# Average pooling 2x2: store packets grown from 16 KB to 63.5 KB per partition, and moved from a queue of their own into the loads' queue

## Chip, cores, metric

The kernel runs on one core of one Trainium2 chip; the other cores are idle. The metric is the device time of one execution in microseconds. All timed runs quoted here are in the fast state, and the core's clock is 1.0 in all of them, so no run had to be set aside; the four probes ran once each, so their state is unknown. The runs were spread over several chips; the kernel before, timed beside each batch, stayed at 3106.4 to 3106.5 us. Ratios are the mean time of one kernel's runs over the mean of the other's in the same rounds, with a 95% interval; they are not quite the ratio of the medians that are quoted. The span of a profile is about 1.7 us shorter than the time of the same execution.

## The reference

```python
x: float32 [32, 128, 256, 256]; kernel_size = 2; stride = 2
for i in range(128):
    for j in range(128):
        output[:, :, i, j] = mean(x[:, :, 2*i:2*i+2, 2*j:2*j+2], axis=(2, 3))
```

1,073.7 MB are read and 268.4 MB are written. Two input rows (2 KB) give one output row (512 bytes); I call this a unit. There are 4,096 units for each of the 128 partitions. A packet is what one DMA engine moves at a time: here one partition's share of a transfer, so a transfer has 128 packets, eight for each of the 16 engines (a load takes 19.3 us, one of its packets 2.42).

## The kernel before

The input is one list of units. A load takes 32 units for each partition: 64 KB per partition, 8 MB in all, one block in HBM. VectorE (DVE) adds the row pairs in place, then the column pairs; ScalarE (ACT) multiplies by 0.25; the result, 16 KB per partition, is stored. Loads are issued by SyncE (SP), stores by ACT: two hardware queues, which share the core's 16 DMA engines.

```python
sbuf = ctx.enter_context(tc.tile_pool(name="sbuf", bufs=2))
for parts in plan:                       # 126 whole loads, then a cut-up tail
    in_tile = sbuf.tile([P, G_MAIN, s * w], f32, name="in_tile")   # 64 KB
    for g in parts:
        xt = xv[r0 : r0 + rows].rearrange("(p g) f -> p g f", p=P)
        ot = ov[r0 : r0 + rows].rearrange("(p g) f -> p g f", p=P)
        ...                              # it = this part of in_tile
        nc.sync.dma_start(out=it, in_=xt)
        nc.vector.tensor_add(...)        # row pairs, in place   (L87)
        col_sum = sbuf.tile([P, G_MAIN, w_out], f32, name="col_sum", bufs=3)
        nc.vector.tensor_add(...)        # column pairs          (L96)
        nc.scalar.mul(out=col_sum[:, :g], in_=col_sum[:, :g], mul=inv)   # L108
        nc.scalar.dma_start(out=ot, in_=col_sum[:, :g])
```

## Time and profile before

| | before |
|---|---|
| time, median of 4 runs | 3106.39 us (3106.34 to 3106.69) |
| span of the profile | 3104.8 us |
| DMA over the span | 432 GB/s |
| one period (load, store, compute) | 24.2 us for 10.49 MB |
| DVE and ACT for one load | 8.69 + 4.43 us, and 3.62 us |

From the page of the kernel before: the engines' busy time, what DMA moved in each fortieth of the span, the two queues, and the three costliest groups (busy time and mean of one, then the idle time before them and what ended it).

```profile
span 3104.8 us, 1126 instructions
DVE 1681.4 (54%) x272; ACT 465.8 (15%) x137; POOL 0.2 (0%) x4
...
GB/s 418 436 439 425 436 439 425 436 438 429 433 439 430 431 439 434 427 439 435 426 438 436 427 437 436 428 436 437 427 436 437 428 436 437 429 435 437 432 431 396
...
q1 hardware_dynamic: 19584, 1073.75, 79.8%
q10 hardware_dynamic: 19584, 268.44, 20.2%
...
L87 DVE TENSOR_TENSOR in_tile<-in_tile 128x8192 f32<-128x8192 f32 (+4 forms) x136 | 1113.9, 8190 | 1406.7 <-DMA in_tile<-in_x_dram 1406.7
L108 ACT ACTIVATE col_sum<-col_sum 128x4096 f32<-128x4096 f32 (+4 forms) x136 | 464.5, 3415 | 2635.9 <-DVE col_sum L96 2635.9
L96 DVE TENSOR_TENSOR col_sum<-in_tile 128x4096 f32<-128x4096 f32 (+4 forms) x136 | 567.8, 4175 | 13.9 <-DMA out_dram<-col_sum 1.8
```

No slice of DMA is poor, and DVE waits 1,407 us in all for loads: the kernel is bound by DMA. The means of these groups mix shapes; the table has those of the full shape. One period in the timeline (start, duration, then the wait before):

```profile
1010.38 8.69 DVE L87 TENSOR_TENSOR in_tile<-in_tile 128x8192 f32<-128x8192 f32 x1 [10.97 <-DMA in_tile<-in_x_dram]
1019.17 4.43 DVE L96 TENSOR_TENSOR col_sum<-in_tile 128x4096 f32<-128x4096 f32 x1
...
1027.27 0.34 ACTq L110 DMA_DIRECT2D out_dram<-col_sum  x1
1034.57 8.69 DVE L87 TENSOR_TENSOR in_tile<-in_tile 128x8192 f32<-128x8192 f32 x1 [10.97 <-DMA in_tile<-in_x_dram]
```

The row adds start 24.19 us apart, so a load and a store of one period move at 10.49 MB / 24.19 us = 433.5 GB/s. The end of the kernel is poorer. Windows (stretch, length, busy times, clock, DMA share, GB/s):

```profile
3080.00:3090.00 10.00, 6.20 (x4) 1.87 (x2) 0.00 (x0) 1.00 0.99 419
3090.00:3100.00 10.00, 7.23 (x8) 2.33 (x4) 0.00 (x0) 1.00 0.82 332
3100.00:3104.80 4.80, 0.58 (x2) 0.63 (x3) 0.00 (x0) 1.00 0.33 111
```

In the last 24.8 us DMA moves (419 x 10 + 332 x 10 + 111 x 4.8) = 8.0 MB, worth 18.5 us at 435.2 GB/s (the most that the prediction below reckons with; it says where the figure comes from): 6.3 us are lost there. This view counts each packet whole in the window in which it starts, so short windows err at their edges.

### The profile page before, as it was taken

The page shows a single profiled execution, that of the slowest core. Times are in us where ns is not written, and L with a number is a line of the kernel's source. Part 1 is how long each engine was busy: PE and PEld are TensorE (multiplying, and loading weights), DVE is VectorE, ACT ScalarE, POOL GpSimd, SP SyncE. Part 2 cuts the span into 40 slices and gives each one's busy share as a digit, 9 for nine tenths or more (in the row PEclk, how much of TensorE's full clock was granted, in tenths as well). Part 3 has the DMA queues.
Part 4 walks back from the last instruction along what each step waited for, and adds up shares of the span by engine and source line. Part 5 has one row for each costly group of instructions (what it writes and reads, how often), then busy time and mean ns, then how long its engine had stood idle before and what let it go on. Part 6 is the DMA issues. An engine that isn't in the chain of part 4 may idle for free. (4 is left out here: it accounts for less than half of the span.)

```text
span 3104.8 us, 1126 instructions
## 1 busy us (share of the span) xinstructions
DVE 1681.4 (54%) x272; ACT 465.8 (15%) x137; POOL 0.2 (0%) x4
## 2 busy tenths in 40 slices
DVE  4555555555555555555555555555555555555556
ACT  1111111111111111111111111111111111111112
POOL 0000000000000000000000000000000000000000
DMA  9999999999999999999999999999999999999999
GB/s 418 436 439 425 436 439 425 436 438 429 433 439 430 431 439 434 427 439 435 426 438 436 427 437 436 428 436 437 427 436 437 428 436 437 429 435 437 432 431 396
DMA packets 39176, 1342.26 MB, mean 432 GB/s; under 512 B 4352, under 2 KB 4736, under 8 KB 5888
## 3 DMA queue, kind: packets, MB, share of 16 engines
q1 hardware_dynamic: 19584, 1073.75, 79.8%
q10 hardware_dynamic: 19584, 268.44, 20.2%
q14 instruction: 8, 0.07, 0.0%
HBM read 1073.74 MB, written 268.44 MB: 432 GB/s over the span
## 5 line engine op out<-in xcount | busy, mean ns | idle before, releaser
L87 DVE TENSOR_TENSOR in_tile<-in_tile 128x8192 f32<-128x8192 f32 (+4 forms) x136 | 1113.9, 8190 | 1406.7 <-DMA in_tile<-in_x_dram 1406.7
L108 ACT ACTIVATE col_sum<-col_sum 128x4096 f32<-128x4096 f32 (+4 forms) x136 | 464.5, 3415 | 2635.9 <-DVE col_sum L96 2635.9
L96 DVE TENSOR_TENSOR col_sum<-in_tile 128x4096 f32<-128x4096 f32 (+4 forms) x136 | 567.8, 4175 | 13.9 <-DMA out_dram<-col_sum 1.8
L108 ACT ACT_TABLE_LOAD x1 | 1.3, 1283 | 0.7 <-PEq L190 0.7
L190 POOL MEMSET const-bfloat16-1.0<- 128x1 bf16 x1 | 0.1, 102 | 0.0
L190 POOL MEMSET const-uint8-127<- 128x1 uint8 x1 | 0.1, 102 | 0.0
L190 POOL MEMSET const-float32-0.0<- 128x1 f32 x1 | 0.1, 99 | 0.2 <-issue 0.2
L190 POOL MEMSET const-float32-1.0<- 128x1 f32 x1 | 0.1, 99 | 0.0
## 6 DMA issues: line engine op xcount, KB each, us to landing
out_dram<-col_sum ACTq DMA_DIRECT2D x126, 2048.0 KB, 31.6
in_tile<-in_x_dram SPq DMA_DIRECT2D x5, 2048.0 KB, 27.5
in_tile<-in_x_dram SPq DMA_DIRECT2D x1, 4096.0 KB, 25.5
out_dram<-col_sum ACTq DMA_DIRECT2D x5, 512.0 KB, 12.0
in_tile<-in_x_dram SPq DMA_DIRECT2D x126, 35.1
out_dram<-col_sum ACTq DMA_DIRECT2D x1, 1024.0 KB, 12.7
in_tile<-in_x_dram SPq DMA_DIRECT2D x1, 1024.0 KB, 16.2
in_tile<-in_x_dram SPq DMA_DIRECT2D x1, 512.0 KB, 16.9
```

What stands on the lines that cost most here:

```text
L87: nc.vector.tensor_add(out=it[:, :, 0:w], in0=it[:, :, 0:w], in1=it[:, :, di * w : (di + 1) * w],)
L96: nc.vector.tensor_add(out=col_sum[:, :g], in0=it[:, :, 0:wu:s], in1=it[:, :, 1 : wu + 1 : s],)
L108: nc.scalar.mul(out=col_sum[:, :g], in_=col_sum[:, :g], mul=inv)
L190: nc = _bacc.Bacc("TRN2", target_bir_lowering=False, num_devices=1)
```

## The change

The intent: fewer and larger transfers, each in one direction for some 19 us, with no small stores mixed in packet by packet; and a tail whose compute hides beside the last big store. A group is now 127 units, loaded in four pieces of 31, 32, 32 and 32 units. All results of a group gather in one buffer and leave as one store of 63.5 KB per partition. To make that one run in HBM, a partition owns 127 units in a row, so the rows that one load reads lie 254 KB apart; before they lay 64 KB apart. The store goes into SP's queue behind the next group's first load, by when its data are ready. The diff, cut to its core:

```diff
-    for parts in plan:
-            nc.sync.dma_start(out=it, in_=xt)
-            ...
-            nc.scalar.dma_start(out=ot, in_=col_sum[:, :g])
+IN_UNITS = 32
+GROUP = 127
+FIRST = GROUP - 3 * IN_UNITS            # 31
+    res = out_pool.tile([P, GROUP + FIRST, w_out], f32, name="res")
+    for k in range(groups):              # 32 groups
+        xt = xv[r0 : r0 + GROUP * P].rearrange("(p g) f -> p g f", p=P)
+        ot = ov[r0 : r0 + GROUP * P].rearrange("(p g) f -> p g f", p=P)
+        base = 0 if k % 2 == 0 else FIRST
+        ...                              # pieces of the group, first the one of 31 units
+        for i, (a, g) in enumerate(pieces):
+            t = in_pool.tile([P, IN_UNITS, 2 * w], f32, name="in_tile")
+            nc.sync.dma_start(out=t[:, :g], in_=xt[:, a : a + g])
+            if i == 0 and last:
+                nc.sync.dma_start(out=last[0], in_=last[1])
+            pool(t[:, :g], res[:, base + a : base + a + g], [g] if i < 3 else [g - 8, 8])
+        last = (ot, res[:, base : base + GROUP])
+    ...   # tail, 32 units: three loads, then the last big store on SP, then
+          # compute and three small stores on ACT's queue beside it
```

More of the change, by code (lines that the diff above doesn't have):

```diff
@@ L27 @@
     R = n * c * h_out
-    if k == s and 2 <= k <= 4 and R > 0 and R % P == 0:
-        _nonoverlap_pool(ctx, tc, x, out, k, n, c, h, w, h_out, w_out)
+    units = R // P if R % P == 0 else 0
+    if k == 2 and s == 2 and h % 2 == 0 and w == 256 and units >= 1024:
+        _pool_2x2(ctx, tc, x, out, units)
     else:
         _generic_pool(ctx, tc, x, out, k, s, n, c, h, w, h_out, w_out)
-def _nonoverlap_pool(ctx, tc, x, out, k, n, c, h, w, h_out, w_out):
+IN_UNITS = 32
+GROUP = 127
+FIRST = GROUP - 3 * IN_UNITS
@@ L36, in _nonoverlap_pool, with _pool_2x2 @@
+def _pool_2x2(ctx, tc, x, out, units):
     nc = tc.nc
     P = nc.NUM_PARTITIONS
-    s = k
-    R = n * c * h_out
-    hv = h_out * s
-    xs = x if hv == h else x[:, :, 0:hv, :]
-    xv = xs.rearrange("n c (ho a) w -> (n c ho) (a w)", a=s)
-    ov = out.rearrange("n c ho wo -> (n c ho) wo")
-    assert xv.shape == (R, s * w) and ov.shape == (R, w_out)
-    wu = w_out * s
-    unit_bytes = s * w * 4
-    G_MAIN = max(1, min(R // P, (64 * 1024) // unit_bytes))
-    total_units = R // P
-    nmain, rem_units = divmod(total_units, G_MAIN)
@@ L54, in _nonoverlap_pool @@
-    plan: list[list[int]] = [[G_MAIN] for _ in range(nmain)]
-    if rem_units:
-        plan.append([rem_units])
-    if G_MAIN % 32 == 0 and nmain >= 4 and rem_units == 0:
-        u = G_MAIN // 32
-        tail = [
-            [16 * u, 8 * u, 8 * u],
-            [8 * u, 8 * u, 8 * u, 4 * u, 2 * u, u, u],
-        ]
-        assert all(sum(t) == G_MAIN for t in tail)
-        plan = plan[:-2] + tail
-    sbuf = ctx.enter_context(tc.tile_pool(name="sbuf", bufs=2))
-    inv = 1.0 / float(k * k)
@@ L71, in _nonoverlap_pool @@
-    r0 = 0
-    for parts in plan:
-        in_tile = sbuf.tile([P, G_MAIN, s * w], mybir.dt.float32, name="in_tile")
-        g0 = 0
-        for g in parts:
-            rows = P * g
-            xt = xv[r0 : r0 + rows].rearrange("(p g) f -> p g f", p=P)
-            ot = ov[r0 : r0 + rows].rearrange("(p g) f -> p g f", p=P)
-            r0 += rows
-            it = in_tile[:, g0 : g0 + g]
-            g0 += g
-            nc.sync.dma_start(out=it, in_=xt)
-            for di in range(1, k):
-                nc.vector.tensor_add(
-                    out=it[:, :, 0:w],
-                    in0=it[:, :, 0:w],
-                    in1=it[:, :, di * w : (di + 1) * w],
-                )
-            col_sum = sbuf.tile(
-                [P, G_MAIN, w_out], mybir.dt.float32, name="col_sum", bufs=3
-            )
-            nc.vector.tensor_add(
-                out=col_sum[:, :g],
-                in0=it[:, :, 0:wu:s],
-                in1=it[:, :, 1 : wu + 1 : s],
-            )
-            for dj in range(2, k):
-                nc.vector.tensor_add(
-                    out=col_sum[:, :g],
-                    in0=col_sum[:, :g],
-                    in1=it[:, :, dj : wu + dj : s],
-                )
-            nc.scalar.mul(out=col_sum[:, :g], in_=col_sum[:, :g], mul=inv)
-            nc.scalar.dma_start(out=ot, in_=col_sum[:, :g])
-        assert g0 <= G_MAIN
@@ L113, in _nonoverlap_pool, with pool @@
-    assert r0 == R, (r0, R)
+    f32 = mybir.dt.float32
+    w = x.shape[3]
+    w_out = w // 2
+    xv = x.rearrange("n c (ho a) w -> (n c ho) (a w)", a=2)
+    ov = out.rearrange("n c ho wo -> (n c ho) wo")
+    in_pool = ctx.enter_context(tc.tile_pool(name="inp", bufs=2))
+    out_pool = ctx.enter_context(tc.tile_pool(name="outp", bufs=1))
+    res = out_pool.tile([P, GROUP + FIRST, w_out], f32, name="res")
+    def pool(it, dst, cuts):
+        nc.vector.tensor_add(out=it[:, :, 0:w], in0=it[:, :, 0:w], in1=it[:, :, w:])
+        a = 0
+        for g in cuts:
+            d, v = dst[:, a : a + g], it[:, a : a + g]
+            nc.vector.tensor_add(out=d, in0=v[:, :, 0:w:2], in1=v[:, :, 1:w:2])
+            nc.scalar.mul(out=d, in_=d, mul=0.25)
+            a += g
@@ new lines, in _pool_2x2 @@
+    groups, rest = divmod(units, GROUP)
+    if rest == 0:
+        groups, rest = groups - 1, GROUP
+    last = None
+    for k in range(groups):
+        r0 = k * GROUP * P
+        xt = xv[r0 : r0 + GROUP * P].rearrange("(p g) f -> p g f", p=P)
+        ot = ov[r0 : r0 + GROUP * P].rearrange("(p g) f -> p g f", p=P)
+        base = 0 if k % 2 == 0 else FIRST
+        spans = [(FIRST + i * IN_UNITS, IN_UNITS) for i in range(3)]
+        if base == 0:
+            pieces = [(0, FIRST)] + spans
+        else:
+            pieces = [(3 * IN_UNITS, FIRST)] + [(a - FIRST, g) for a, g in spans]
+        for i, (a, g) in enumerate(pieces):
[5 more added lines that the diff above has]
+        last = (ot, res[:, base : base + GROUP])
@@ new lines, in _pool_2x2 @@
+    r0 = groups * GROUP * P
+    while rest:
+        n = min(rest, IN_UNITS)
+        t = in_pool.tile([P, IN_UNITS, 2 * w], f32, name="in_tile")
+        tout = in_pool.tile([P, IN_UNITS, 2 * w], f32, name="in_tile")
+        to = tout[:].rearrange("p g f -> p (g f)").rearrange("p (g f) -> p g f", f=w_out)
+        cuts = [n // 2, n // 4, n - n // 2 - n // 4] if n >= 8 else [n]
+        a, parts = 0, []
+        for g in cuts:
+            xt = xv[r0 : r0 + g * P].rearrange("(p g) f -> p g f", p=P)
+            ot = ov[r0 : r0 + g * P].rearrange("(p g) f -> p g f", p=P)
+            nc.sync.dma_start(out=t[:, a : a + g], in_=xt)
+            parts.append((ot, a, g))
+            a += g
+            r0 += g * P
+        rest -= n
+        if rest == 0:
+            nc.sync.dma_start(out=last[0], in_=last[1])
+        for ot, a, g in parts:
+            pool(t[:, a : a + g], to[:, a : a + g], [g])
+            nc.scalar.dma_start(out=ot, in_=to[:, a : a + g])
```

## The prediction

> **What bounds the kernel now.** The DMA engines, throughout. The page's 40 slices show DMA at 9 tenths everywhere, mean 432 GB/s; DVE is busy 54%, ACT 15%. By shape, an 8 MB load costs DVE 8.69 + 4.43 us and ACT 3.62 us; the timeline repeats every 24.20 us (row adds at 66.85 and 3043.27 us are 123 periods apart), of which DVE waits 11 us for a load. A period moves 8.389 + 2.097 MB: 433.3 GB/s. The Trainium skill, "DMA: Bandwidth & Descriptors", section "Where 436 GB/s comes from", puts the ceiling at 435.2. The trace agrees: the second load, no store beside it, lands 19.32 us after the first (42.02 - 22.70), 434.2 GB/s. In the packets, 64 KB take 2.418 us and 16 KB 0.611 us: 27.2 GB/s per engine plus about 9 ns a packet. All bytes at 435.2 GB/s need an estimated 3084 us, so no schedule wins more than some 20 us (0.7%).
>
> **Where those 20 us are.** 3.4 us before the first load flows and lands (22.70 - 19.32); about 13 us of packet cost (24.20 against 24.09 us a period; some 6 ns for each of 34,800 data packets); about 5 us at the end, where the windows 3090 to 3100 and 3100 to 3105 us show DMA shares of 0.82 and 0.31.
>
> **What the change does.** Loads stay 64 KB per partition (one in four 62 KB). Stores grow from 16 to 63.5 KB: store packets fall from 16,128 to 4,096, all data packets to about 21,200. At 6 to 9 ns over 16 engines that saves 5 to 7 us. Bytes and compute are unchanged; DVE and ACT have slack.
>
> *Does the one queue run dry?* Let a group's last load land at T. DVE needs 13.1 us, ACT's last call (8 units) 1.06: the store can be issued at T + 15. The next group's first load, issued at about T - 6, occupies the engines until T + 18.7, so the store is some 4 us early. The load behind it needs a buffer freed at T + 13.5, and the store runs until T + 38. I see no starved moment.
>
> *Tail.* The last big store needs about 19 us of DMA; the last compute (2.3 + 1.2 + 1.1 us) and the small stores (2 MB) hide beside it. Some 3.5 of the 5 us come back.
>
> **Sum, an estimate.** A group of 127 units: 41.6 MB / 435.2 GB/s = 95.64 us, + 40 packets x 6 ns = 95.9. Then 3.4 + 32 x 95.9 + 24.2 (rest) + 1.5 (last landing) + 1.6 (time over span before) = 3099.5 us. The saving is on the critical path, but only about 7 us, 0.2%.
>
> **Predicted: 3099 us, 3093 to 3106.** Faster by over 2%: 0.5%; within 2%: 98%; slower by over 2%: 1.5%.
>
> **What would show it.** Right: about 95.9 us per group; 63.5 KB packets of about 2.40 us; DMA share near 1.0 until 2 or 3 us before the end; stores issued before the running load ends. Wrong, step by step: 16 KB pieces still in the packets; a DMA gap at each change from load to store; a tail still waiting for DVE.
>
> **What would make it wrong.** Each of about 64 changes of direction in one queue costs something (0.15 us each would eat the gain); pure stores to HBM are slower than the mix (this trace has no long pure store); loads at a 254 KB pitch instead of 64 KB lose rate; or the store waits longer for ACT and stops the loads behind it.

## The result, and the profile after

| | before | after |
|---|---|---|
| time, median of 4 runs | 3106.39 us | 3114.76 us (3112.14 to 3114.97) |
| ratio | | 1.0025 (1.0011 to 1.0039) |
| span | 3104.8 us | 3113.1 us |

The time stayed within 2%, as forecast, but rose by 8 us where a fall by 7 us was predicted, and it lies outside the stated range of 3093 to 3106 us. From the page of the changed kernel, the same lines as before, and the sizes of the transfers (KB each, median us from issue to landing):

```profile
span 3113.1 us, 927 instructions
DVE 1681.9 (54%) x294; ACT 467.7 (15%) x164; POOL 0.2 (0%) x4
...
GB/s 428 427 438 429 439 430 430 427 440 427 433 436 429 428 437 430 431 427 439 429 428 436 432 429 430 437 429 428 428 427 439 432 427 439 429 437 433 429 427 417
...
q1 hardware_dynamic: 23472, 1340.09, 99.8%
q10 hardware_dynamic: 432, 2.10, 0.2%
...
L60 DVE TENSOR_TENSOR in_tile<-in_tile 128x8192 f32<-128x8192 f32 (+2 forms) x131 | 1113.0, 8497 | 1402.1 <-DMA in_tile<-in_x_dram 1402.1
L65 ACT ACTIVATE res<-res 128x4096 f32<-128x4096 f32 (+3 forms) x160 | 462.4, 2909 | 2619.6 <-DVE res L64 2619.6
L64 DVE TENSOR_TENSOR res<-in_tile 128x4096 f32<-128x4096 f32 (+3 forms) x160 | 564.4, 3544 | 10.8 <-DVE in_tile L60 0.5
...
out_dram<-res SPq DMA_DIRECT2D x32, 8128.0 KB, 22.0
```

Packets fell from 39,168 to 23,904 (34,816 and 21,248 of them carry data, the others have 4 bytes) and everything but the tail runs in one queue, as meant. Compute is the same. The page's DMA lines alone don't show where 8 us went; the timeline does. It is enough to look at the starts of the row adds, each of which waits for one load. First a group that is nearly at full rate, then one of the worst (losses of 0.12 and 0.97 us by the reckoning below, where the whole range is 0.12 to 1.05):

```profile
96.12 0.35 SPq L88 DMA_DIRECT2D out_dram<-res  x1
...
99.02 8.43 DVE L60 TENSOR_TENSOR in_tile<-in_tile 128x7936 f32<-128x7936 f32 x1 [5.53 <-DMA in_tile<-in_x_dram]
...
137.56 8.69 DVE L60 TENSOR_TENSOR in_tile<-in_tile 128x8192 f32<-128x8192 f32 x1 [25.79 <-DMA in_tile<-in_x_dram]
...
156.92 8.69 DVE L60 TENSOR_TENSOR in_tile<-in_tile 128x8192 f32<-128x8192 f32 x1 [6.15 <-DMA in_tile<-in_x_dram]
...
965.55 8.43 DVE L60 TENSOR_TENSOR in_tile<-in_tile 128x7936 f32<-128x7936 f32 x1 [5.46 <-DMA in_tile<-in_x_dram]
...
1005.14 8.69 DVE L60 TENSOR_TENSOR in_tile<-in_tile 128x8192 f32<-128x8192 f32 x1 [26.84 <-DMA in_tile<-in_x_dram]
...
1024.47 8.69 DVE L60 TENSOR_TENSOR in_tile<-in_tile 128x8192 f32<-128x8192 f32 x1 [6.12 <-DMA in_tile<-in_x_dram]
```

Between the row adds of the first and second load of a group stand one store and one load, 16.7 MB, worth 38.40 us at 435.2 GB/s. The good group took 38.54 us, the bad one 39.59 us. The load that follows without a store took 19.36 and 19.33 us, which is full rate. The windows of both stretches and of the end say the same:

```profile
99.02:137.56 38.54, 12.72 (x2) 3.51 (x1) 0.00 (x0) 1.00 1.00 434
965.55:1005.14 39.59, 12.72 (x3) 3.51 (x1) 0.00 (x0) 1.00 0.99 422
...
3085.00:3095.00 10.00, 9.87 (x6) 2.97 (x2) 0.00 (x0) 1.00 1.09 468
3095.00:3105.00 10.00, 0.00 (x0) 1.06 (x1) 0.00 (x0) 1.00 1.05 454
3105.00:3113.10 8.10, 0.00 (x0) 0.00 (x0) 0.00 (x0) 1.00 0.52 217
```

Note the DMA share of 0.99 in the bad stretch: a packet that takes longer counts as busy all that time, so the share hides the loss and only the GB/s show it. At the end 11.0 MB move in 28.1 us, worth 25.2 us: 2.9 us lost. Here too the edges err: 468 and 454 GB/s become 430 and 434 when packets are cut at the edges of their windows, and the loss becomes 2.6 us, against 6.6 before. The tail gave back 4.0 us, where 3.5 were predicted.

**The loss by place.** The trace has every DMA packet. I take, for each transfer, the mean of the midpoints of its 128 packets; from one transfer to the next that distance, less the bytes at 435.2 GB/s and 6 ns a packet, is what an average engine lost between them:

```
                    places   mean loss   sum
load  -> load         96      0.01 us     1.2 us
load  -> store        31      0.03 us     0.9 us
store -> load         31      0.45 us    13.8 us
a whole group (from its last load to the next group's last load): 31 x 0.51 = 15.9 us
```

Span less this loss is 3113.1 - 15.9 = 3097.2 us. The prediction's sum was 3099.5 - 1.6 = 3097.9 us of span. So its other terms held as a sum (single ones may cancel), and one is missing. The expectations below still have 0.465 us for the change from store to load, where this table has 0.45. In the packets themselves the loss is the last store packet, 2.69 us on average in place of 2.40, and the first load packet, 2.58 in place of 2.42. Here are six of the 16 engines at one such change, that of the third store (durations in us of the last two store packets and of the first load packet, engines in the order in which they got there; the trace does not name engines, so a packet is put down to the engine whose last one ended as it began):

```
engine   store 7   store 8   load 1
1st        2.40      2.88      2.47
2nd        2.40      3.02      2.42
5th        2.40      3.07      2.42
7th        2.40      2.59      2.80
10th       2.40      2.40      2.42
16th       2.40      2.40      2.42
```

Within a store or a load nearly every packet has its full rate. Only at the change some engines lose 0.2 to 0.7 us, here the ones that come first. At others nearly all lose (at 981 us all 16 last store packets are longer than 2.40 us); the longest single packets are 3.48 us (store) and 3.51 us (load). DVE does nothing within 2.7 us of any of the 31 changes, and ACT is busy there for 1.0 us of 5.4 on average (3.0 in run e2 below, which loses less), so compute that runs at that very moment does not explain it.

### The profile page after: what moved, and what is told of

It reads as the page before. It is cut to its first block, busy times and chain, and to the rows that moved or that the text cites. A ratio compares the mean times of both kernels' runs of the same rounds, so it can differ in the third digit from the quotient of the medians.

```text
span 3113.1 us, 927 instructions
## 1 busy us (share of the span) xinstructions
DVE 1681.9 (54%) x294; ACT 467.7 (15%) x164; POOL 0.2 (0%) x4
## 4 chain that ended last, share of the span: by engine, by line
DMA 69%; DVE 26%; ACT 4%; SPq 0%; issue 0%; DVEq 0%
DMA in_tile<-in_x_dram 69%; DVE in_tile L60 18%; DVE res L64 8%; ACT res L65 4%; SPq L88 0%; DVE in_tile L64 0%; DVEq L64 0%; ACT in_tile L65 0%; SPq L86 0%
## 5 line engine op out<-in xcount | busy, mean ns | idle before, releaser
L60 DVE TENSOR_TENSOR in_tile<-in_tile 128x8192 f32<-128x8192 f32 (+2 forms) x131 | 1113.0, 8497 | 1402.1 <-DMA in_tile<-in_x_dram 1402.1
L65 ACT ACTIVATE res<-res 128x4096 f32<-128x4096 f32 (+3 forms) x160 | 462.4, 2909 | 2619.6 <-DVE res L64 2619.6
L64 DVE TENSOR_TENSOR res<-in_tile 128x4096 f32<-128x4096 f32 (+3 forms) x160 | 564.4, 3544 | 10.8 <-DVE in_tile L60 0.5
## 6 DMA issues: line engine op xcount, KB each, us to landing
out_dram<-in_tile ACTq DMA_DIRECT2D x1, 1024.0 KB, 19.6
```

The lines of the kernel that those rows point to most:

```text
L60: nc.vector.tensor_add(out=it[:, :, 0:w], in0=it[:, :, 0:w], in1=it[:, :, w:])
L64: nc.vector.tensor_add(out=d, in0=v[:, :, 0:w:2], in1=v[:, :, 1:w:2])
L65: nc.scalar.mul(out=d, in_=d, mul=0.25)
```

## The experiments

The four probes (p1 to p4) and e9, e10 and e12 give a wrong result; all others give the reference's result. Three measures recur. "Loss" is that of a whole group, as above. "Apart" is how far the first and the last of the 16 engines are from each other at a group's last load. "Ahead" is the time from the issue of a store's first part to the start of its first packet on the earliest engine; the smallest value seen is 0.84 us, which I take to be that of an engine already idle. All three come from the one profiled run of each kernel. Runs of one kernel in one queue differ by up to 7 us (e7), which is 0.24 us a group, so small differences in loss between two kernels say nothing.

### 1. The big stores in the other queue: e1_act_queue

```diff
             if i == 0 and last:
-                nc.sync.dma_start(out=last[0], in_=last[1])
+                nc.scalar.dma_start(out=last[0], in_=last[1])
```

> The big stores go into the other hardware queue (issued by ACT), nothing else changes: still 63.5 KB packets, the same tail. Theory T (the loss sits where one queue passes from a store to a load, 0.465 us on each of 31 such places in the changed kernel): with loads already waiting in their own queue there is nothing to lose there, so 3114.8 - 14.4 = 3100 us, 3097 to 3103, and the loads around a store land without excess. Rival A (63.5 KB stores or loads at a 254 KB pitch are slow in themselves, or the lengths collide in HBM): stays at 3113 to 3115. Rival B (mixing loads and stores packet by packet is what costs, as the change's author may have thought): over 3115.

Measured: 3313.38 us, 6.7% over the kernel before (1.0654 to 1.0686). Theory T and rival A missed (T's 14 us could not be seen under so much other loss); rival B (over 3115) had the direction, but no size, and 200 us were on nobody's list. Issue to landing, and windows that end with the row add of a group's second load, while the store runs: the first store, and the seventh, with a later window and the timeline beside it:

```profile
out_dram<-res ACTq DMA_DIRECT2D x31, 8128.0 KB, 47.2
```

```profile
112.11:148.32 36.21, 0.00 (x0) 3.51 (x1) 0.00 (x0) 1.00 0.95 357
733.98:765.23 31.25, 0.00 (x1) 3.51 (x1) 0.00 (x0) 1.00 1.01 433
775.50:779.40 3.90, 2.94 (x1) 0.93 (x1) 0.00 (x0) 1.00 0.08 34
```

```profile
765.23 8.69 DVE L60 TENSOR_TENSOR in_tile<-in_tile 128x8192 f32<-128x8192 f32 x1 [31.28 <-DMA in_tile<-in_x_dram]
774.01 4.43 DVE L64 TENSOR_TENSOR res<-in_tile 128x4096 f32<-128x4096 f32 x1
778.46 0.33 SPq L86 DMA_DIRECT2D in_tile<-in_x_dram  x1
```

The 357 GB/s of the first store, with load packets of up to 4.4 us in place of 2.42, are the exception: with packets cut at the edges, DMA moves 361 GB/s during the first store and 419 to 429 during each of the other 30. The time goes after the store. In the group shown the second load lands only at 765.2 us, with the end of the store. From 775.5 us on most engines have no packet of the third load left, and the fourth waits for a buffer until DVE has done with the second, at 778.4: the queue runs dry, with as few as one packet in flight and 34 GB/s. Over the trace, engines without a packet lose as much as 110 us of all 16 engines would be (0.9 us in the changed kernel), and packets that are longer than usual 103 us (17 in the changed kernel; of the 3.3 us a store only 0.4 fall while the store runs). Together that is some 195 of the 199 us. The Trainium skill, "DMA: Bandwidth & Descriptors", section "Issuing engines are not separate DMA queues", says that transfers of different issuers interleave on the same 16 engines, and that several issuers only save issue time. Here the choice of queue, with the same bytes and packets, changed the time by 3313.38 - 3114.76 = 199 us; the measurement decides.

### 2 and 3. The store in two halves, together and apart: e2_split_together, e3_split_apart

```diff
             if i == 0 and last:
-                nc.sync.dma_start(out=last[0], in_=last[1])
+                nc.sync.dma_start(out=last[0][:, :64], in_=last[1][:, :64])
+            if i == 0 and last:          # e3: i == 1, behind the second load
+                nc.sync.dma_start(out=last[0][:, 64:], in_=last[1][:, 64:])
```

> Each big store is issued as two, one directly behind the other, in the same queue: the number of passes from store to load stays 31, the number of stores that end doubles. Theory T1 (the first reads of a load from HBM are what is waited for, when the queue had been reading SBUF): 3115 to 3117 us (4,000 more packets at 6 ns over 16 engines are 1.5 us) and no stretched packet between the two halves. Rival T2 (every end of a store waits for its writes to land in HBM): another 31 x 0.465 = 14.4 us, about 3130 us, with stretched packets between the halves.

> The two halves of each big store are placed behind the next group's first and second load: passes from store to load double to 62, bytes and packets are those of e2. T1 and T2 alike: e2 is exceeded by 31 x 0.465 = 14.4 us under T1 (about 3130 us) and not at all under T2 (both about 3130 us). A rival that lays the loss on the one store that comes late for its slot (it was issued under 3 us before the running load landed) expects no more loss from the second half: about 3116 us.

Measured: 3105.81 us (e2) and 3109.62 us (e3), both faster than the changed kernel. T1 and T2 fall together: e3 has 62 changes from store to load and loses 0.23 us a group, less than half of what the changed kernel loses with 31; e2 ends 62 stores in the queue and loses 0.12. A change of direction has no fixed price of its own, and neither has the end of a store. The third theory in e3's text, the late store, wanted about 3116 us and missed too.

### 4. Transfers alone, small stores: p1_probe

> Wrong result on purpose: no pooling, only transfers from one source tile, in stretches of one queue: loads alone (32 KB per partition), load and store in turn (stores 16 KB), load and copy inside SBUF in turn (12 KB), stores alone, copy and store in turn, load-store-copy in turn, and load and store in two queues. Loss at a place where one transfer ends and the next begins, from the packets (gap, and stretch of the last and first packet over the median). T1 (a load's first HBM reads are exposed after a transfer that read SBUF): store to load 0.4 to 0.5 us, copy to load the same, all other pairs under 0.05. T2 (HBM writes draining): store to load, store to store and store to copy 0.4 to 0.5, copy to load near 0. Rival A (63.5 KB, odd alignment): near 0 everywhere, as all sizes here are powers of two or 12 KB.

Measured, as loss of a whole pair or triple in its stretch: load and store 0.02 us, load and copy 0.05, copy and store none, load-store-copy 0.03. No pair of kinds costs anything at these sizes and without compute. Two stretches could not be read: the stores of the other queue had nothing to wait for, so they were issued at the very start, into the stretch of loads alone.

### 5 to 7. Which packet stands before the load: e4_small_last, e5_small_first, e6_four

```diff
-                nc.sync.dma_start(out=last[0], in_=last[1])
+                for a, e in ((0, 111), (111, 127)):   # e4;  e5: (0, 16), (16, 127)
+                    nc.sync.dma_start(out=last[0][:, a:e], in_=last[1][:, a:e])
+                # e6: four parts of 32, 32, 32 and 31 units
```

> Each big store is issued as 111 + 16 units (55.5 KB, then 8 KB per partition), directly one behind the other in the same queue. Theory P (after the first four runs: what is lost where a queue passes from a store to a load grows with the size of the store's packet just before the load: none seen at 16 KB, about 0.1 us at 32 KB, 0.465 us at 63.5 KB): with 8 KB packets before the load nothing is lost; 4,096 more packets are 1.5 us, so 3101 to 3103 us. Rival Q (any second store helps, because it lets the engines drift apart, wherever the cut is): about 3105 us here and in the next run alike, as with two halves.

> The same cut the other way round: 16 units first, then 111, so that packets of 55.5 KB stand before the load. Theory P: almost the loss of the changed kernel, 3111 to 3115 us. Rival Q: about 3105 us, like the run before.

> Each big store as four of about 16 KB per partition, directly one behind the other. Theory P: no loss at the change, 12,288 more packets at 6 ns over 16 engines are 4.6 us: 3104 to 3106 us, no better than two halves. Rival Q: the more pieces, the more drift, and the cost of packets is the same: not told apart by this run alone.

Measured: 3122.03, 3108.86 and 3113.20 us. Theory P falls, with the sign reversed: 8 KB packets before the load (e4) lose 0.68 us a group, 55.5 KB packets there (e5) 0.24. Rival Q fell with it, since it wanted both at 3105. Cutting a store also lets its first part go earlier. In e5, e6 and the halves that part needs only early pieces of the group and is issued as soon as those are done: ahead 17.8 to 21.5 us. In e4 the first part still needs the last piece: ahead 1.5 us. So e4 and e5 differ in two things, the packet before the load and the lead of the first part.

### 8. Sizes, transfers alone: p2_sizes

> Wrong result on purpose: transfers only, one queue, pairs repeated eight times: a 64 KB load and a store of 63.5, 48, 32, 16 or 8 KB per partition; a 16 KB load and a 63.5 KB store; a 64 KB load and a copy of 63.5 KB inside SBUF; a 64 KB load and stores of 55.5 and 8 KB; a 64 KB load and a 63.5 KB store whose rows lie 64 KB apart; 63.5 KB stores alone. Loss of a pair = its period less bytes at 435.2 GB/s less 6 ns a packet. Theory P: about 0.45, 0.3, 0.1, 0, 0 us for the five store sizes, 0.45 with the small load, 0 for 55.5 and 8 KB, 0.45 at the 64 KB pitch, 0 for stores alone. For the copy inside SBUF 0.45 if it is the change of source that counts, 0 if writes to HBM must come before. Rival H (the odd pitch of the rows in HBM): the 64 KB pitch shows no loss.

Measured: with 63.5 KB stores the first pair lost 1.05 us, the following ones 0.02 to 0.12, while the engines moved apart from 1 us to over 3 us. 48 and 32 KB lost 0.07 and 0.02 us, smaller ones nothing, rows 64 KB apart nothing, 55.5 and 8 KB nothing after a first 0.5, stores alone nothing once running. So a 63.5 KB store next to a 64 KB load runs at full rate in one queue; P and H both fall. Only the first stretch began with the engines together, however; in the others they were already 2 to 18 us apart, so these do not compare the sizes fairly. Only the copy inside SBUF was slow: 8.3 us lost for each pair.

### 9 and 10. An early store, and only the first store cut: e7_store_later, e8_first_split

```diff
-            if i == 0 and last:
+            if i == 1 and last:          # e7
                 nc.sync.dma_start(out=last[0], in_=last[1])
```

e8 has the two halves of e2 for the first store of the loop and whole stores for the other 30.

> The big store is placed behind the next group's second load instead of the first; nothing else changes (63.5 KB packets, one queue, as many changes of direction). So it is issued some 22 us before its turn instead of 3. Theory D (drift: engines lose time at a change when all 16 make it nearly together; in the probe of sizes they drifted apart by several us within a few changes and then lost nothing; in the kernel the store comes about 3 us before its turn, so no engine can run ahead further than that): with the store early the engines can drift, the loss fades after a few groups: 3099 to 3104 us, the span of a load over its packets grows beyond 2.4 us. Rival A (the rows of the loads, 254 KB apart in HBM, collide with the stores' rows at a change): no change, 3112 to 3116 us.

> Only the first of the 31 stores inside the loop is issued as two halves, all others whole. Theory D: the first change then costs about 1 us and leaves the engines 2.3 us apart, as in the run with all stores halved, and if that state keeps itself the rest of the kernel loses little: about 3102 to 3106 us. If each halving is needed: 3113 to 3116 us. Rival A: 3113 to 3116 us.

Measured: 3113.44 us (3108.29 to 3115.62, the widest of the one-queue runs) and 3115.73 us. In e8 the first change lost 0.56 us and left the engines 0.8 us apart, at the next group 1.45, and they stayed near there: 0.55 us a group afterwards. In e7 the store is 19.5 us ahead and the engines are 2.65 us apart, as theory D wanted, and still 0.44 us a group are lost, now from load to store (0.25) and between the two loads before it (0.15), with 0.01 from store to load. Theory D falls as a sufficient cause. Of all runs this one alone gives a whole store more lead, and its times overlap those of the changed kernel (3112.14 to 3114.97).

### 11. Distance of the rows, transfers alone: p3_pitch

> Wrong result on purpose, transfers only. One queue: four loads and a 63.5 KB store behind the first, with the loads' rows 254 KB apart (A) and 64 KB apart (B). Two queues, a load and a store running side by side: loads at 254 KB with stores of 63.5 KB (C), loads at 64 KB with stores of 63.5 KB (D), loads at 64 KB with stores of 16 KB (E), loads at 254 KB with stores of 16 KB (F). Theory D: A and B lose alike, about 1 us at the first change and then under 0.1; C to F are for the 3313 us of the two-queue run: if size of the store's packet matters there, C and D lose alike and E and F nothing. Rival A: A loses about 0.45 us at every change and B nothing; C and F are slow, D and E at full rate.

Inconclusive as planned: again the stores of the other queue did not wait for the loads that they were meant to accompany. Those of 63.5 KB ran one after another from 27 to 1220 us, over stretches A and B. One thing can be read: in the first four groups of A a 63.5 KB store ran beside every 64 KB load without a break, and each transfer of the first queue was delayed by 19.2 to 19.3 us (one by 19.6, one at the edge by less), where the store's own bytes are worth 19.1. Long packets in two queues side by side can go at full rate, as they nearly do in e1 after its first store; here nothing waits for compute, so no engine runs out of work.

### 12 to 15. Distance of the rows in the kernel: e9_dense_loads, e10_two_queues_dense, e11_group112, e12_stores_64k

```diff
-            nc.sync.dma_start(out=t[:, :g], in_=xt[:, a : a + g])
+            rd = r0 + a * P              # e9, e10: one block, rows 64 KB apart
+            xd = xv[rd : rd + g * P].rearrange("(p g) f -> p g f", p=P)
+            nc.sync.dma_start(out=t[:, :g], in_=xd)
-GROUP = 127
+GROUP = 112                              # e11 alone
-        ot = ov[r0 : r0 + GROUP * P].rearrange("(p g) f -> p g f", p=P)
+        ot = ov[k * 128 * P : (k + 1) * 128 * P].rearrange(       # e12 alone
+            "(p g) f -> p g f", p=P)[:, :GROUP]
```

e10 has e1's line as well.

> Wrong result on purpose: each load fetches the same number of rows as in the changed kernel, but from one block, so that its partitions lie 64 KB apart in HBM, as in the kernel before, and not 254 KB. Stores, order, queue, waits and compute are those of the changed kernel. Theory A (the rows that a load reads at once, 254 KB apart, collide with the store's rows around a change): the loss of 0.5 us a change goes, 3098 to 3102 us. Theory D (16 engines changing at nearly the same moment lose time wherever the rows lie): 3112 to 3116 us.

> Wrong result on purpose: the loads of the run before, and the big stores in the other hardware queue as in the run that took 3313 us. Theory A: loads and stores no longer collide while they run side by side, 3097 to 3105 us. Theory D: the mixing itself costs, still about 3313 us.

> Groups of 112 units in place of 127, a correct kernel: loads' rows 224 KB apart, stores of 56 KB per partition, 36 groups and 35 changes. Theory D: about as the changed kernel and a little more, 3113 to 3118 us. Theory A: another distance of the rows, another loss; its size cannot be told in advance, but a value well outside 3110 to 3120 would speak for it.

> Wrong result on purpose: the 63.5 KB stores go to rows 64 KB apart in HBM in place of 63.5 KB (30 of 31 stores in the loop); loads as in the changed kernel. Theory A: the stores' distance is the other half of the pair, the loss changes clearly, in one direction or the other (outside 3110 to 3118 us). Theory D: 3112 to 3116 us.

Measured: 3110.51, 3310.77, 3392.20 and 3119.49 us. Theory A falls as the main cause: dense loads lose 0.35 us a group in place of 0.51, and in two queues they change nothing. With other rows of the stores (e12) it is 0.62, and all four times lie above those of the changed kernel, so the rows of the stores have some part in its size. For the loads' rows that is not shown: the runs of e9 go from 3109.14 to 3115.11 us and overlap those of the changed kernel, and the 0.35 are from the fastest of them.

e11 tests nothing of the sort. With 112 units the first load has 16 units and takes 9.7 us, while the next transfer has to wait 13 us for DVE to free a buffer. Here the queue does run dry; windows of e11 around that moment:

```profile
905.00:912.00 7.00, 6.29 (x1) 0.00 (x0) 0.00 (x0) 1.00 1.04 449
912.00:917.00 5.00, 4.90 (x2) 0.00 (x0) 0.00 (x0) 1.00 0.12 52
917.00:922.00 5.00, 5.00 (x3) 3.71 (x2) 0.00 (x0) 1.00 0.60 210
```

### 16. Small stores in the other queue: e13_two_queues_16k

```diff
-                nc.sync.dma_start(out=last[0], in_=last[1])
+                for c in range(0, GROUP, 32):
+                    e = min(c + 32, GROUP)
+                    nc.scalar.dma_start(out=last[0][:, c:e], in_=last[1][:, c:e])
```

> The two-queue kernel that took 3313 us, with each big store issued as four of 16 KB per partition, as the kernel before stores. If it is the long store packets beside long load packets that cost 200 us there: 3102 to 3108 us (3097 us with no loss, 4.6 us for the packets, 1.6 us over the span). If the rest of that kernel is to blame (groups, one buffer for results, loads' rows 254 KB apart): still over 3250 us.

Measured: 3104.58 us (3104.40 to 3104.85), the fastest of all, ratio to the kernel before 0.9994 (0.9977 to 1.0011). This lies in the range that was expected if long store packets are to blame. So the groups, the one buffer for results and the 254 KB rows of e1 are not by themselves what cost 200 us. The edit did two things, however: each quarter went out as soon as its data were ready, so one small store runs beside each load, as in the kernel before. From the timeline of e13, one store a load:

```profile
1015.84 0.34 ACTq L90 DMA_DIRECT2D out_dram<-res  x1
1023.12 8.69 DVE L60 TENSOR_TENSOR in_tile<-in_tile 128x8192 f32<-128x8192 f32 x1 [10.96 <-DMA in_tile<-in_x_dram]
...
1040.01 0.34 ACTq L90 DMA_DIRECT2D out_dram<-res  x1
1047.31 8.69 DVE L60 TENSOR_TENSOR in_tile<-in_tile 128x8192 f32<-128x8192 f32 x1 [10.97 <-DMA in_tile<-in_x_dram]
```

The row adds are 24.19 us apart, the period of the kernel before. Whether e1 suffered from the length of its store packets or from its stores coming in bursts, this run does not part; the trace of e1 above puts its loss after the store and not into the mixing itself.

### 17. The loads in halves: e14_load_halves

```diff
-            nc.sync.dma_start(out=t[:, :g], in_=xt[:, a : a + g])
+            nc.sync.dma_start(out=t[:, :16], in_=xt[:, a : a + 16])
+            nc.sync.dma_start(out=t[:, 16:g], in_=xt[:, a + 16 : a + g])
```

> One queue, whole stores of 63.5 KB as in the changed kernel; each load is issued as two of about 32 KB per partition. 16,384 more packets cost about 6 us. Theory E (nearly equal long packets on both sides keep the 16 engines in one arrangement, in which they lose about 0.5 us at each change; other lengths on either side let them settle in another): the loss falls below 0.15 us a change, about 3104 to 3108 us. If only the store's packets matter: 3119 to 3123 us.

Measured: 3124.74 us, loss 0.64 us a group. Theory E falls: shorter load packets do not help.

### 18. The same order of transfers, no compute: p4_no_compute

> Wrong result on purpose, transfers only, one queue, the changed kernel's order (four loads, the 63.5 KB store behind the first), so no transfer waits for compute: with its rows of 254 KB (A), with rows of 64 KB (B), with the store in two pieces (C). If the loss comes from the transfers alone: about 0.5 us a change in A, less in B (the dense run had 0.35), under 0.15 in C. If it takes the kernel's waits (the store's late issue, buffers freed by compute): it fades after a few changes in A and B, as in the probe of sizes.

Measured: in A the first change lost 1.2 us, then a whole group lost 0.09 us; in B 0.08, in C 0.05. The very transfers that lose 0.51 us a group in the changed kernel, in the same order and queue, lose next to nothing without compute. The loss needs the kernel's waits or its compute; since hardly any compute runs at the changes (see above), the waits are likelier, but no run shows it. Without them the engines moved 2.4 us apart at the first change and stayed so.

### All one-queue runs side by side

| run | time, us | loss a group, us | apart, us | ahead, us |
|---|---|---|---|---|
| p4, A: no compute | | 0.09 | 2.7 | 33.6 |
| e2: halves | 3105.81 | 0.12 | 2.7 | 18.0 |
| e3: halves, apart | 3109.62 | 0.23 | 3.1 | 17.8 |
| e5: 16 + 111 | 3108.86 | 0.24 | 2.7 | 21.5 |
| e6: four | 3113.20 | 0.28 | 3.0 | 21.2 |
| e9: dense loads | 3110.51 | 0.35 | 1.0 | 1.4 |
| e7: behind the second load | 3113.44 | 0.44 | 2.7 | 19.5 |
| the change | 3114.76 | 0.51 | 1.2 | 1.3 |
| e8: first store cut | 3115.73 | 0.55 | 1.2 | 1.2 |
| e12: stores' rows 64 KB apart | 3119.49 | 0.62 | 1.3 | 1.2 |
| e14: loads in halves | 3124.74 | 0.64 | 1.2 | 1.2 |
| e4: 111 + 16 | 3122.03 | 0.68 | 1.6 | 1.5 |

For every timed row, span less 31 times the loss less the packets' cost (6 ns for each packet more than the change has, over 16 engines) gives 3096.6 to 3098.4 us. So this one loss accounts for the differences between all these times.

The time is the median and the rest is from the profiled run, which is up to 1.4 us faster (e9). The rows fall into two classes, with one exception. Where a store comes just in time (ahead 1.2 to 1.5 us), the engines stay within 1 to 1.6 us of each other and lose 0.35 to 0.68 us a group; where its first part comes early, they are 2.7 to 3.1 us apart and lose 0.09 to 0.28. e4 against e5 is the closest pair: the same two pieces and packets, in the other order. e7 is the exception: early and apart, yet 0.44. So lateness of the store goes with the loss, but I have not shown that it makes it; the one run that changes lateness alone, e7, speaks against it.

## Why the prediction was wrong

- **What bounds the kernel: right.** DMA, in both; DVE waits 1,407 and 1,402 us for loads.
- **Bytes, packets, start: right as a sum.** The Trainium skill's ceiling of 435.2 GB/s ("DMA: Bandwidth & Descriptors", "Where 436 GB/s comes from") agrees with 434 GB/s in a loads-only trace stretch, and the sum built on it came within 1 us of the span once the loss is taken off (3097.9 against 3097.2).
- **Tail: right.** 4.0 us came back; 3.5 were predicted.
- **Does the one queue run dry: nearly right, and tighter than thought.** The store was to come 4 us early. In the group shown it is issued 2.9 us before the row add that waits for the load ahead of it (96.12 and 99.02), and on average the earliest engine starts it 1.3 us after its issue, in some groups after 0.84 us, so it had been waiting. That wait itself costs little: 0.03 us from load to store, and engines without a packet add up to 0.9 us in the whole loop.
- **The step that failed is the sum:** "A group of 127 units: 41.6 MB / 435.2 GB/s = 95.64 us, + 40 packets x 6 ns = 95.9." The groups took 96.4 us: (3029.40 - 137.56) / 30 between the same row add of groups 1 and 31. The missing 0.5 us stand at the changes from store to load. The text named such a cost among its doubts, put the break-even at 0.15 us for each of 64 changes, and gave it no share in the number: the figure for a queue that carries both directions was taken from a trace in which none does. It measured 0.45 us from store to load, 0.03 from load to store.
- **The words "change of direction" were wrong as well,** as a cause: e2 and e3 have as many changes or more and lose less, and in p1, p2 and p4 hardly anything is lost at a change after the first.

So the step that failed is shown; its deeper cause is not. What stays open: which of the kernel's waits, or its compute, brings the loss about, and why e7 has it; what makes a late store cost at its end and not at its beginning; how the rows' distance in HBM enters; and in e1, which loses some 7 us a store ((3311.9 - 3097.2) / 31), why a load's last packets come so late and why packets are longer after the store. Told apart so far for the one queue: none of these alone makes the loss: the change of direction, the end of a store, the size of the packet before the load, the length of load packets, or the same transfers without the kernel's waits and compute.

No version is clearly better than the kernel before. e13 is 0.06% faster in the mean and within noise of the same by its interval; by the prediction's estimate of 3084 us at most 0.7% could be had.

## What to carry to other kernels

When the data path is at 99% of its measured rate, a change that moves the same bytes in another order can win only tenths of a per cent, and a few tenths of a microsecond at each of 31 places are enough to turn it into a loss; measure such a cost before building on a plan without it, and measure it inside the kernel, since transfers alone showed 0.09 us a group where the kernel had 0.51. Cutting a store so that a first part can go early took the loss from 0.51 to between 0.12 and 0.28 us a group here; giving the whole store a load's worth of lead (e7: 0.44) did not clearly help, so try it and measure. Putting large stores into a second queue beside large loads is not a neutral choice: it cost 6% here, over half of it because a load came late and the next one waited for its buffer, and small stores, one beside each load, cost nothing. Look at how many packets are in flight after such a store, and not only while it runs.

## What the Trainium skill lacked or had wrong

- "DMA: Bandwidth & Descriptors", "Rules for kernel authors", asks for at least 1 MiB per DMA for bandwidth. All transfers of the main loops here are larger; still larger was not better: in two queues 8 MB stores took 3313.38 us where 2 MB stores took 3104.58 (e1 and e13, which differ in when the stores go, too). I found no page that names a size above which larger transfers stop helping, or a cost where stores and loads meet.
- The same page, "Issuing engines are not separate DMA queues": that the choice of issuer only saves issue time did not hold; 3114.76 against 3313.38 us for the same transfers.
- The same page, "Latency and other measured facts", has about 0.6 us to the first byte for transfers issued by SP or ACT. It does not say from when. In these traces the first packet of the first load starts 1.0 us after the issuing instruction starts and 0.64 us after it ends, so counted from its end the figure agrees.
- No page has that the 16 engines can move apart, or that a pair of a load and a store can cost up to 1 us (1.05 us for the first pair of the probe of sizes, 0.02 to 0.12 for the next six, while the engines moved from 1 to 3 us apart). Whether the second depends on the first is not shown.
- No page has that a copy inside SBUF with 63.5 KB packets, alternating with 64 KB loads, is slow: 8.3 us lost for each pair, its packets 2.4 to 4.3 us long, half of them 3.7 or more, in place of 2.4 (with the engines 8 to 20 us apart). With 12 KB packets it ran at full rate.
